# Modulation vectors made in the layer that uses them, and a feed-forward sum that is gated at its end

## The chip, the cores and the metric

The kernel runs on one core of a Trainium2 chip. The metric is the device time of one execution in microseconds (us), as the median of the runs shown. The engines are TensorE (PE, with its weight loads as PEld), VectorE (DVE), ScalarE (ACT), GpSimd (POOL) and SyncE (SP), whose queue issues all the DMAs that are spoken of here.

## What is computed

Two layers over 5 tiles of 128 tokens (one tile of context, four of latent tokens), 1024 wide. The reference of one layer, cut to what matters here:

```python
m = silu(cond) @ w_ada + b_ada
sh1, sc1, g1, sh2, sc2, g2 = split(m, 6)
h = layer_norm(x) * (1 + sc1) + sh1
o = mixing(h)            # state space | neighbourhood attention | grouped-query attention, then w_out
x = layer_norm(ALPHA * x + g1 * o, ln1_g, ln1_b)
h = layer_norm(x) * (1 + sc2) + sh2
a, gate = split(h @ w_ffn_in, 2)
f = (silu(a) * gate) @ w_ffn_out
x = layer_norm(ALPHA * x + g2 * f, ln2_g, ln2_b)
```

The context tile and the latent tiles have a conditioning vector each, so m has two rows. The six vectors of m are numbered 0 to 5 (sh1, sc1, g1, sh2, sc2, g2); "half" 0 or 1 is the first or last 512 columns of one.

## The kernel before

Matrix products are made in three matmuls of split operands (`mm3`, lines 311 to 313); `wload` and `wsplit` load a weight block by DMA into a buffer of the tag `wr` (three of them) and split it, a copy on ACT (line 283) and a subtraction on POOL or DVE (line 284), into buffers of the tags `wh` and `wl` (seven of each).

The order of the work is written as Python generators that a loop advances by tables of counts; a scheduler then orders each engine's instructions by priority and readiness. The stages of a layer are:

1. Mixers (`layer`, lines 1370 to 1448). 18 attention units of the grouped-query stage run in `pipelined`; after unit n the function `between` advances the state space mixer (`SSMN`), the remaining input projections (`WINN`) and the modulation (`ADAN`: one vector half after each of the units 6 to 11). Then follow 10 units of the neighbourhood attention.
2. Output projection (`wout`): two groups of tiles; after the second, `ADAW` advances three modulation steps. For each tile follow LayerNorm (`post_ln`), normalisation and the transposed input of the network. `xs[i]` is the tile after LayerNorm, in a `k4` buffer.
3. Feed-forward network (`ffn`): 22 column blocks f in six parts, `PARTS = (4, 4, 4, 3, 4, 3)`. Each block is `ffn_in` (products of 320 columns). After its blocks a part makes ten products of 512 columns (five tiles, two halves), each in one PSUM bank of `psA`, which takes the tags psM and psT in turn, two banks each. A product is multiplied by the gate row g2 (line 1755) and added to ALPHA * `xs[i]` (line 1757, part 0) or to `xs[i]` (line 1762). From f = 2 on, every block also advances `ffn_side` by one step: one modulation half (`ada_side`) and one step of the tables for the next layer's state space mixer (`ssm_tables`, lines 615 to 664).

One half of a modulation vector (`ada`, lines 361 to 401) loads eight row blocks of w_ada, 256 KB each, makes 32 matmuls (64 rows of the trace) into one PSUM bank, copies the bank's 128 columns on ACT (line 385), transposes the copy (line 386) and adds the bias on DVE (line 391 or 393). In the mixers the weights come two blocks at a time through `wr`; beside the network one at a time through `ev`, four buffers. For the gates the two rows go to DRAM (line 401), and `bcast_row` (line 406) reads them back to all partitions.

Layer 0's vectors 0 and 1 are made at the program's start, its vectors 2 to 4 in its mixers through the list `todo`. All later halves come from `ada_side`: vector 5 of the same layer, then vectors 0 to 4 of the next one, so that layer 1 has nothing to make in its mixers. That is 12 halves in layer 0, three in `wout` and nine beside the blocks f = 2 to 10.

## Time and profile before

| | us |
|---|---|
| median of 3 runs | 1804.81 |
| lowest and highest run | 1793.88, 1805.54 |
| the profiled execution | 1804.75 |
| its span, first to last instruction | 1802.7 |

Rough stages in the profiled execution: layer 0's mixers to 396 us, its projection to 460, its network to 990; layer 1's mixers to 1281, its projection to 1350, its network to the end. The parts of a network are cut where the sum of a part's last product begins (line 1762).

How to read the rows: a row of a table of windows has the stretch (start:end), its length, then for PE, PEld, DVE, ACT and POOL the busy us with the number of instructions, the mean granted clock of TensorE as a share of 2.4 GHz, the share of time in which the DMA engines are busy, and GB/s. A window taken for one line has PE and PEld of that line alone. A row of a group of instructions has line, engine, operation, result and operands, shape and count, then busy us and mean ns of one, then the idle time of the engine just before them and what ended it. A row of one line's instructions has the count, then the duration in ns (least, median, most), and the first and last start. Names such as wa, ev, psM are the tiles of the program.

### The profile page before, as it was taken

Reading aid. Unit: us, or ns where it says so; the run is one execution under the profiler, and the core shown is the slowest. Engines: PE = TensorE matmul, PEld = TensorE weight load, DVE = VectorE, ACT = ScalarE, POOL = GpSimd, SP = SyncE. Lnnn points to the kernel's source line nnn. Section 1 sums busy time; section 2 is a strip of 40 time slices with the busy share of each in tenths; the row PEclk is TensorE's granted clock in tenths of the full one; section 3 lists DMA queues with packets and bytes.
Section 4 is the critical chain, followed back from the end, with each engine's and each line's share of the span. In section 5 each row is a group of like instructions: output and inputs, shape, how many; then the busy total and the mean of one; then the engine's idle time right before and its main releaser. Section 6 shows DMA issues by size and latency. Waiting matters only on the chain.

```text
span 1802.7 us, 31473 instructions
## 1 busy us (share of the span) xinstructions
PE 1655.2 (92%) x11624; PEld 1447.3 (80%) x11624; DVE 1224.2 (68%) x2460; ACT 822.3 (46%) x1796; POOL 762.5 (42%) x651
## 2 busy tenths in 40 slices
PE   5889899898899999999898989998979999999997
PEld 3778677676688888898797978976759898998995
DVE  5576536646778777678877555565476787876777
ACT  5435445556542334243246446665564342432433
POOL 3753303048434334346266232210684464363453
PEclk8889899889899999999999989998989999999999
DMA  8434767545453545332324243463542232222312
GB/s 311 121 110 116 231 202 203 149 158 178 149 161 115 176 126 184 109 115 72 122 77 165 91 115 86 121 183 113 178 161 83 91 98 64 89 74 68 105 60 82
DMA packets 183114, 234.90 MB, mean 130 GB/s; under 512 B 78960, under 2 KB 112048, under 8 KB 182960
## 3 DMA queue, kind: packets, MB, share of 16 engines
q1 hardware_dynamic: 182960, 232.88, 42.3%
q8 instruction: 92, 1.51, 0.3%
q14 instruction: 62, 0.51, 0.1%
HBM read 203.57 MB, written 29.39 MB: 129 GB/s over the span
## 4 chain that ended last, share of the span: by engine, by line
PE 66%; DVE 12%; DMA 10%; ACT 4%; issue 3%; POOL 2%; SPq 1%; POOLq 0%; DVEq 0%; ACTq 0%
PE psM L311 9%; PE psM L312 9%; PE psM L313 9%; PE psT L311 6%; PE psT L312 6%; PE psT L313 5%; DMA ev<-in_w_ada_dram 3%; PE psT L859 3%; PE psS L311 2%; PE psS L312 2%; PE psS L313 2%; PE psS L1157 2%; DMA wr<-in_w_ffn_in_dram 2%; PE psT L1184 2%; POOL wl L284 2%
## 5 line engine op out<-in xcount | busy, mean ns | idle before, releaser
L284 POOL TENSOR_TENSOR wl<-wr,wh 128x512 fp32r<-128x512 f32 x362 | 502.1, 1406 | 523.8 <-ACT wh L283 341.6
L283 ACT CAST wh<-wr 128x512 fp32r<-128x512 f32 x450 | 275.0, 620 | 388.4 <-PE psM L313 91.3
L311 PE MATMUL psM<-hh,wh 128*128 128x320 f32 x560 | 178.1, 318 | 2.5 <-DVE ev L400 1.2
L312 PE MATMUL psM<-hl,wh 128*128 128x320 f32 x560 | 176.2, 315 | 0.3 <-POOL hl L284 0.3
L313 PE MATMUL psM<-hh,wl 128*128 128x320 f32 x560 | 176.2, 315 | 0.0
L311 PEld LDWEIGHTS psM<-hh,wh 128*128 128x128 f32 x560 | 107.1, 191 | 5.5 <-DVE ev L400 1.8
L311 PE MATMUL psT<-hh,wh 128*128 128x320 f32 x352 | 110.0, 312 | 0.0
L312 PE MATMUL psT<-hl,wh 128*128 128x320 f32 x352 | 109.1, 310 | 0.0
L313 PE MATMUL psT<-hh,wl 128*128 128x320 f32 x352 | 109.0, 310 | 0.0
L313 PEld LDWEIGHTS psM<-hh,wl 128*128 128x128 f32 x560 | 107.0, 191 | 1.7 <-issue 1.6
L312 PEld LDWEIGHTS psM<-hl,wh 128*128 128x128 f32 x560 | 107.2, 191 | 1.1 <-POOL hl L284 0.6
L230 POOL TENSOR_TENSOR sm<-sm,mhalf 128x1 f32<-128x1 f32 (+2 forms) x46 | 55.9, 1217 | 96.3 <-DVE sm L260 51.7
L1638 DVE TENSOR_TENSOR ys<-ys,psM 128x320 f32<-128x320 f32 x140 | 65.0, 482 | 34.7 <-PE psM L313 32.9
L1638 DVE TENSOR_TENSOR ys<-ys,psT 128x320 f32<-128x320 f32 x140 | 65.1, 481 | 30.4 <-PE psT L313 29.0
L1160 DVE TENSOR_REDUCE psS<-psS 128x1 f32<-128x640 f32 x64 | 52.8, 828 | 45.3 <-PE psS L1157 43.7
L311 PE MATMUL psT<-b,wh 128*128 128x320 f32 x240 | 76.6, 319 | 7.3 <-DVE ys L1638 7.2
L311 PE MATMUL psM<-b,wh 128*128 128x320 f32 x240 | 76.4, 318 | 5.7 <-DVE ys L1638 5.6
L284 POOL TENSOR_TENSOR wl<-ws,wh 128x512 fp32r<-128x512 f32 x40 | 53.6, 1341 | 62.7 <-ACT wh L283 62.6
L311 PE MATMUL psM<-wh,hh 128*128 128x256 f32 (+1 forms) x232 | 73.8, 318 | 6.1 <-DVE sm L1329 2.9
L311 PE MATMUL psM<-wh,xs 128*128 128x512 f32 x190 | 75.1, 395 | 3.5 <-DVE k L1762 2.8
L311 PE MATMUL psT<-wh,xs 128*128 128x512 f32 x190 | 75.3, 396 | 2.9 <-DVE k L1762 2.9
L859 PE MATMUL psT<-ident,ys 128*128 128x128 f32 x440 | 75.4, 291 | 2.7 <-ACT ys L290 1.0
(439 smaller groups left out, 4904.8 us busy)
## 6 DMA issues: line engine op xcount, KB each, us to landing
wr<-in_w_ffn_in_dram SPq DMA_DIRECT2D x88, 512.0 KB, 3.8
ev<-in_w_ada_dram SPq DMA_DIRECT2D x112, 256.0 KB, 4.0
wr<-in_w_ffn_out_dram SPq DMA_DIRECT2D x40, 512.0 KB, 3.9
wr<-in_w_out_dram SPq DMA_DIRECT2D x32, 512.0 KB, 3.6
wr<-in_w_in_dram SPq DMA_DIRECT2D x28, 512.0 KB, 4.4
wa<-in_w_ada_dram SPq DMA_DIRECT2D x24, 512.0 KB, 4.6
k<-in_x_dram SPq DMA_DIRECT2D x10, 512.0 KB, 5.6
xs<-zqk SPq DMA_DIRECT2D x32, 160.0 KB, 5.1
```

Of the source, the lines that this page charges most:

```text
L230: self.nc.gpsimd.tensor_tensor(out=o, in0=v, in1=self.mhalf.broadcast_to([128, v.shape[1]]), op=ALU.pow)
L283: nc.scalar.copy(hi, src)
L284: (lo_eng or nc.vector).tensor_tensor(out=lo, in0=src, in1=hi.bitcast(F32), op=ALU.subtract)
L311: nc.tensor.matmul(ps, lhsT=ah, rhs=bh, start=first, stop=False)
L312: nc.tensor.matmul(ps, lhsT=ah, rhs=bl, start=False, stop=False)
L313: nc.tensor.matmul(ps, lhsT=al, rhs=bh, start=False, stop=last)
L859: self.nc.tensor.transpose(pt[:, j * 128:(j + 1) * 128], s, self.ident)
L1157: nc.tensor.matmul(sp[:, b, 0:320], lhsT=qT[:, h * 128:(h + 1) * 128], rhs=kx[kv][:, b * 320:(b + 1) * 320], start=st, stop=en)
L1160: V.tensor_reduce(out=m, in_=sp[:, :, 0:320], axis=AX.XY, op=ALU.max, negate=True)
L1184: nc.tensor.matmul(pt[hh * 64:hh * 64 + 64, 256:384], lhsT=K["v"][:, j, kv * 64:kv * 64 + 64], rhs=PTs[j // 2][:, c0:c0 + 128], start=(j = ...
L1638: V.tensor_tensor(out=o, in0=x, in1=y, op=ALU.add)
```

## The change

Four edits go together.

- Vectors 2 to 4 of each layer are made in that layer's own mixers (`todo` is filled anew for each layer), and `ada_side` makes only vectors 0 and 1 of the next layer. Beside layer 0's network three halves are left (f = 2 to 4).
- In the mixers the new generator `ada_parts` makes a half in parts. A step of it computes the part whose weights the step before loaded, and loads the next. A part has two blocks of w_ada in the grouped-query stage, through `wr`, and up to four in the neighbourhood stage, through the buffers `wh` and `wl`. Each part has its own PSUM bank, ACT copy, transpose and DVE addition into `modc`. With 13 steps after the units 5 to 17 and up to 11 beside the neighbourhood units that makes 19 parts for a layer.
- The network's sum starts from zero, not from ALPHA * x, and without the gate: part 0 is copied by ACT, parts 1 to 3 are added by DVE. Part 4 fetches x from DRAM, in a buffer of the tag `zt` (two of them), adds, multiplies by the gate and adds ALPHA * x. Part 5 is as before.
- To that end every tile after LayerNorm is stored to a DRAM tile `xd` in `wout`. The gate rows are read when part 4 first needs them.

```diff
-    ADAN = (0,) * 6 + (1,) * 6 + (0,) * 6
+    ADA0 = 5
...
+    def ada_parts(self, l, M, todo):
...
+        for vec, half in todo:
+            c0 = vec * D + half * 512
+            mc = modc[:, vec, half * 4:half * 4 + 4, :]
+            k0 = 0
+            while k0 < KD:
+
+                n = 4 if self.ada_free else 2
+                n = min(n, KD - k0)
+                if self.ada_free:
+                    raws = [self.wp.tile([128, 512], F32, name=self.nm("wa"), tag=("wh", "wl")[j % 2], bufs=self.NW)
+                            for j in range(n)]
+                    for j, raw in enumerate(raws):
+                        nc.sync.dma_start(raw, wv[:, k0 + j, c0:c0 + 512])
+                else:
+                    raw = self.wp.tile([128, n, 512], F32, name=self.nm("wa"), tag="wr", bufs=self.NRAW)
+                    nc.sync.dma_start(raw, wv[:, k0:k0 + n, c0:c0 + 512])
+                    raws = [raw[:, j] for j in range(n)]
+                yield
+                bank = self.psM()
+                ps, pt = bank[:, 0:128], bank[:, 128:256]
+                for k in range(n):
+                    for j in range(4):
+                        nc.tensor.matmul(ps[32 * j:32 * j + 32, :], lhsT=self.silc[:, k0 + k, :],
+                                         rhs=raws[k][:, j * 128:(j + 1) * 128], start=(k == 0), stop=(k == n - 1),
+                                         tile_position=(0, 32 * j))
+                mrow = self.zt(128)
+                nc.scalar.copy(mrow, ps)
+                nc.tensor.transpose(pt, mrow, self.ident)
...
+                if k0:
+                    nc.vector.tensor_tensor(out=mc, in0=got, in1=mc, op=ALU.add)
+                else:
+                    nc.vector.scalar_tensor_tensor(out=mc, in0=got, scalar=float(vec in (1, 4)), in1=bc, op0=ALU.add,
+                                                   op1=ALU.add)
+                k0 += n
...
-            for _ in range(self.ADAN[n]):
-                if todo:
-                    self.ada(l, M, *todo.pop(0))
+            if n >= self.ADA0:
+                next(ada, None)
...
+        self.ada_free = True
         Ns = [self.na_prep(l, 0, zqk[0], znv)]
...
+            if n:
+                next(ada, None)
-        for _ in ssm:
+        for _ in itertools.chain(ada, ssm):
             pass
...
+                nc.sync.dma_start(xd[i], xs[i])
                 self.ffn_in_tile(xn, i, M["modc"], H)
...
-        for key, cd in (("gp", 0), ("gs", 1)):
-            row(key, M["gates"][1, cd])
...
-                g = row("gp", M["gates"][1, 0]) if i == 0 else row("gs", M["gates"][1, 1])
-                t = ps
-                V.tensor_tensor(out=t, in0=ps, in1=g[:, cs], op=ALU.mult)
+                x = xs[i][:, cs]
                 if part == 0:
-                    V.scalar_tensor_tensor(out=xs[i][:, cs], in0=xs[i][:, cs], scalar=ALPHA, in1=t, op0=ALU.mult,
-                                           op1=ALU.add)
-                elif last:
-                    self.residual(xs[i][:, cs], t, sums[n])
+                    S.copy(x, ps)
+                elif part < len(PARTS) - 2:
+                    V.tensor_tensor(out=x, in0=ps, in1=x, op=ALU.add)
                 else:
-                    V.tensor_tensor(out=xs[i][:, cs], in0=xs[i][:, cs], in1=t, op=ALU.add)
+                    g = row("gp", M["gates"][1, 0]) if i == 0 else row("gs", M["gates"][1, 1])
+                    if last:
+                        V.tensor_tensor(out=ps, in0=ps, in1=g[:, cs], op=ALU.mult)
+                        self.residual(x, ps, sums[n])
+                    else:
+                        t = self.zt()
+                        nc.sync.dma_start(t, xd[i][:, cs])
+                        V.tensor_tensor(out=ps, in0=ps, in1=x, op=ALU.add)
+                        V.tensor_tensor(out=ps, in0=ps, in1=g[:, cs], op=ALU.mult)
+                        V.scalar_tensor_tensor(out=x, in0=t, scalar=ALPHA, in1=ps, op0=ALU.mult, op1=ALU.add)
...
-            for vec in range(5):
+            for vec in range(2):
...
-            todo = [(2 + n // 2, n % 2) for n in range(6)]
             for l in range(L):
+                todo = [(2 + n // 2, n % 2) for n in range(6)]
```

The diff leaves the order of an engine's instructions to the scheduler, so three places of it follow. The first is PE in layer 1's neighbourhood stage, before: L859 and L978 are the transposes and the value products of an attention unit, L853 spreads its sums, L916 and L942 are scores, L767 is the state space mixer.

```order
L859 MATMUL psT_13526<-ident,ys_13339 128x128 x2
L859 MATMUL psT_13578<-ident,ev_13571 128x128 x2
L978 MATMUL psT_13526<-ys_13519,xs_13289 64x128 x4
L978 MATMUL psT_13526<-ys_13519,k_2439_13283 64x128 x2
L853 MATMUL psT_13526<-ident,sm_13355 64x128 x2
L767 MATMUL psS_13626<-k_2464_13374,k_2465_13375 80x128
L942 MATMUL psS_13662<-b_2490_13544,b_2489_13543 128x256
```

And PE at the same place with the change, ahead of the same step of the state space mixer (now L818); L427 and L432 are the matmuls and the transpose of a modulation part, wa its weights.

```order
L427 MATMUL psM_13557<-wa_13505,silc 32x128 x4
L427 MATMUL psM_13557<-wa_13506,silc 32x128 x4
L427 MATMUL psM_13557<-wa_13507,silc 32x128 x4
L427 MATMUL psM_13557<-wa_13508,silc 32x128
L432 MATMUL psM_13492<-ident,zt_13501 128x128
L427 MATMUL psM_13557<-wa_13508,silc 32x128 x3
L818 MATMUL psS_13669<-k_2495_13342,k_2496_13343 80x128 x8
L821 MATMUL psS_13669<-k_2494_13341,k_2220_11888 80x128 x2
L910 MATMUL psT_13652<-ident,ys_13398 128x128 x2
```

A whole part of four blocks has come in between, and the transpose of the part before it, each with a bank psM of its own.

The second place is DVE at the products of part 4 in layer 1, before: one multiplication (L1755) and one addition (L1762) for each product.

```order
L1755 TENSOR_TENSOR psT_18311<-psT_18311,k_2736_14773 128x512
L1755 TENSOR_TENSOR psM_18326<-psM_18326,k_2736_14773 128x512
L1762 TENSOR_TENSOR k_2655_14370<-k_2655_14370,psT_18311 128x512
L1755 TENSOR_TENSOR psT_18341<-psT_18341,k_2735_14771 128x512
L1762 TENSOR_TENSOR k_2653_14367<-k_2653_14367,psM_18326 128x512
L1762 TENSOR_TENSOR k_2575_13975<-k_2575_13975,psT_18341 128x512
L1755 TENSOR_TENSOR psM_18356<-psM_18356,k_2736_14773 128x512
```

And with the change, the same products on DVE: addition (L1821), gate (L1822), and ALPHA * x from the loaded row zt (L1823).

```order
L1821 TENSOR_TENSOR psT_18395<-psT_18395,k_2717_14496 128x512
L1821 TENSOR_TENSOR psM_18415<-psM_18415,k_2715_14493 128x512
L1822 TENSOR_TENSOR psT_18395<-psT_18395,k_3438_18408 128x512
L1821 TENSOR_TENSOR psT_18433<-psT_18433,k_2637_14098 128x512
L1822 TENSOR_TENSOR psM_18415<-psM_18415,k_3438_18408 128x512
L1823 SCALAR_TENSOR_TENSOR k_2717_14496<-zt_18410,psT_18395 128x512
L1822 TENSOR_TENSOR psT_18433<-psT_18433,k_3443_18446 128x512
L1821 TENSOR_TENSOR psM_18453<-psM_18453,k_2635_14095 128x512
L1823 SCALAR_TENSOR_TENSOR k_2715_14493<-zt_18428,psM_18415 128x512
L1822 TENSOR_TENSOR psM_18453<-psM_18453,k_3438_18408 128x512
```

Three instructions stand for a product where two did, and a bank is free after the third.

The third place is the SP queue at the end of layer 0's part 4, before: wr are the weights of the blocks f = 19 (9931, 9933) and f = 20 (10079, 10081).

```order
L1582 DMA wr_9931<-in_w_ffn_in_dram 128x1024
L1582 DMA wr_9933<-in_w_ffn_in_dram 128x1024
L406 DMA k_1976_10493<-in_ln_b_dram 128x1024
L664 DMA tabC_5862<-ev_9729 128x2x256
L664 DMA tabC_5862<-ev_9734 128x2x256
L1582 DMA wr_10079<-in_w_ffn_in_dram 128x1024
L1582 DMA wr_10081<-in_w_ffn_in_dram 128x1024
```

And the SP queue there with the change; wr_9838 and wr_9840 are the weights of f = 20, and zt the rows of x. The first two of the ten row loads stand far ahead, at the network's start.

```order
L715 DMA tabC_5951<-ev_9459 128x2x256
L1820 DMA zt_9539<-xd_4523 128x512
L1820 DMA zt_9557<-xd_4523 128x512
L1820 DMA zt_9575<-xd_4523 128x512
L1639 DMA wr_9838<-in_w_ffn_in_dram 128x1024
L1820 DMA zt_9613<-xd_4523 128x512
L1820 DMA zt_9631<-xd_4523 128x512
L1820 DMA zt_9649<-xd_4523 128x512
L1820 DMA zt_9667<-xd_4523 128x512
L1820 DMA zt_9685<-xd_4523 128x512
L1059 DMA zt_10841<-in_qkg_dram 128x128
L1639 DMA wr_9840<-in_w_ffn_in_dram 128x1024
```

Eight row loads now stand ahead of the second load for f = 20; each of them waits until DVE has freed a buffer zt. A small load of the next stage (L1059) goes into zt as well.

## Rows read from the trace of the kernel before

**Rows 1.** Head of the page: span, and each engine's busy time and share.

```profile
span 1802.7 us, 31473 instructions
PE 1655.2 (92%) x11624; PEld 1447.3 (80%) x11624; DVE 1224.2 (68%) x2460; ACT 822.3 (46%) x1796; POOL 762.5 (42%) x651
```

**Rows 2.** Windows: layer 0's parts 0, 1, 2, 4; layer 1's part 1.

```profile
468.00:565.00 97.00, 90.63 (x660) 80.25 (x660) 72.55 (x194) 38.58 (x76) 32.15 (x25) 0.97 0.43 137
565.00:662.00 97.00, 92.55 (x717) 79.31 (x716) 74.69 (x134) 33.73 (x70) 37.32 (x29) 0.98 0.57 161
662.00:761.00 99.00, 98.86 (x732) 84.50 (x732) 68.08 (x105) 34.21 (x67) 40.38 (x30) 1.00 0.44 135
...
825.00:915.00 90.00, 80.78 (x457) 74.66 (x456) 75.48 (x113) 29.24 (x57) 39.39 (x29) 0.96 0.31 100
...
1437.00:1514.00 77.00, 76.36 (x453) 71.14 (x453) 58.74 (x88) 28.86 (x56) 37.47 (x29) 1.00 0.26 83
```

**Rows 3.** Windows of line 381 alone, layer 0's parts 1 and 2.

```profile
565.00:662.00 97.00, 11.41 (x254) 5.83 (x254) 0.98 0.57 161
662.00:761.00 99.00, 9.88 (x192) 4.09 (x192) 1.00 0.44 135
```

**Rows 4.** Groups of instructions, 565 to 761 us, and line 386's own row.

```profile
L381 PE MATMUL psS<-ev,silc 128*32 128x128 f32 x446 | 21.3, 282 | 4.3 <-DMA ev<-in_w_ada_dram 4.2
...
L386 PE MATMUL psS<-ident,ev x9: 270/272/272, 522.4 to 750.7; 128*128 128x128 f32 x9
```

**Rows 5.** Groups of instructions on PE, 662 to 761 us: the tables.

```profile
L631 PE MATMUL psS<-k,ev 128*128 128x32 f32 x32 | 4.7, 280 | 0.0
...
L655 PE MATMUL psS<-ident,ev 128*128 128x128 f32 x16 | 2.4, 272 | 0.0
```

**Rows 6.** Windows in the mixers of both layers.

```profile
1052.00:1175.00 123.00, 116.95 (x1029) 105.27 (x1030) 69.85 (x185) 76.33 (x196) 27.05 (x35) 0.96 0.38 104
1175.00:1281.00 106.00, 98.39 (x657) 77.02 (x656) 58.66 (x151) 61.80 (x163) 23.38 (x26) 0.89 0.55 160
...
1200.00:1255.00 55.00, 48.23 (x297) 36.45 (x296) 35.19 (x97) 31.37 (x91) 5.67 (x10) 0.78 0.53 145
...
141.00:313.00 172.00, 156.68 (x1588) 134.24 (x1590) 97.44 (x226) 89.16 (x223) 47.72 (x55) 0.97 0.66 193
1067.00:1194.00 127.00, 124.77 (x1141) 112.53 (x1140) 75.71 (x198) 81.58 (x210) 27.54 (x38) 1.00 0.39 107
```

**Rows 7.** Groups on PE, 181 to 276 us: layer 0's six halves.

```profile
L381 PE MATMUL psM<-wa,silc 128*32 128x128 f32 x384 | 18.1, 280 | 5.1 <-DMA wa<-in_w_ada_dram 5.0
...
L386 PE MATMUL psM<-ident,zt 128*128 128x128 f32 x5 | 1.6, 313 | 3.1 <-ACT zt L385 3.1
```

**Rows 8.** Lines 1755 and 1762; window of ten products in layer 1.

```profile
L1755 DVE TENSOR_TENSOR psM<-psM,k x50: 686/695/700, 544.4 to 1730.7; 128x512 f32<-128x512 f32 x50
...
L1762 DVE TENSOR_TENSOR k<-k,psM x40: 628/681/689, 641.4 to 1731.4; 128x512 f32<-128x512 f32 x40
...
1711.00:1731.00 20.00, 20.00 (x91) 16.64 (x90) 15.04 (x22) 4.61 (x8) 5.62 (x5) 1.00 0.08 27
```

**Rows 9.** Loads of w_ada (line 377) to landing; one DMA issue.

```profile
DMA to landing us min/median/max: 2.5/4.4/8.0
...
xmid<-k SPq DMA_DIRECT2D x5, 512.0 KB, 2.6
```

**Rows 10.** POOL's group, 300 to 318 us; window of layer 0's projection.

```profile
L284 POOL TENSOR_TENSOR wl<-wr,wh 128x512 fp32r<-128x512 f32 x4 | 5.5, 1410 | 0.8 <-ACT wh L283 0.8
...
396.00:460.00 64.00, 55.42 (x332) 42.06 (x331) 41.52 (x90) 38.05 (x71) 51.99 (x42) 0.89 0.55 179
```

**Rows 11.** Groups on PE, 141 to 313 us: the tables in layer 0's mixers.

```profile
L631 PE MATMUL psS<-k,k 128*128 128x32 f32 x32 | 4.5, 268 | 0.0
...
L655 PE MATMUL psS<-ident,k 128*128 128x128 f32 x20 | 3.1, 278 | 0.4 <-ACT ev L658 0.4
```

**Rows 12.** Line 381, 396 to 480 us: PE idle before it (us, times).

```profile
  DMA ev<-in_w_ada_dram: 12.1, 7
```

More of the change, by code (lines that the diff above doesn't have):

```diff
@@ L1 @@
+import itertools
 import math
@@ L394, in ada @@
         if vec in (2, 5) and half == 1:
-            gc = self.smallp.tile([128, 2, KD], F32, name=self.nm("gc"), tag="gc", bufs=1)
-            nc.vector.tensor_copy(gc, modc[:, vec].rearrange("p k c -> p c k"))
-            pt = bank[0:16, 256:384]
-            nc.tensor.transpose(pt, gc.rearrange("p c k -> p (c k)"), self.ident)
-            row = (self.ev(n=128) if side else self.zt(128))[0:16]
-            nc.vector.tensor_copy(row, pt)
-            nc.sync.dma_start(gates[vec // 3].rearrange("c (k p) -> (c k) p", p=128), row)
+            self.gate_rows(M, vec, bank, self.ev if side else self.zt)
@@ new lines, in gate_rows @@
+    def gate_rows(self, M, vec, bank, place):
+        nc = self.nc
+        gc = self.smallp.tile([128, 2, KD], F32, name=self.nm("gc"), tag="gc", bufs=1)
+        nc.vector.tensor_copy(gc, M["modc"][:, vec].rearrange("p k c -> p c k"))
+        pt = bank[0:16, 256:384]
+        nc.tensor.transpose(pt, gc.rearrange("p c k -> p (c k)"), self.ident)
+        row = place(n=128)[0:16]
+        nc.vector.tensor_copy(row, pt)
+        nc.sync.dma_start(M["gates"][vec // 3].rearrange("c (k p) -> (c k) p", p=128), row)
@@ L1417, in between @@
                     preps[n + self.AHEAD][0](preps[n + self.AHEAD][1])
+        ada = self.ada_parts(l, M, todo)
         self.pipelined(units, 1, between)
@@ L1470, in wout @@
         ada = self.ada_side(l, M, nxt)
+        xd = self.dp.tile([NT, 128, D], F32, name=self.nm("xd"))
         self.function(AF.Silu, self.after)
```

13 lines of the change are left out of this document (11 added, 2 removed).

## Prediction

> **What bounds the kernel now.** The head of the page says that TensorE (PE) is busy for 1655.2 of 1802.7 us and VectorE (DVE) for 1224.2 [rows 1]. That is a mean over stages, so the windows come next. In layer 1's network, part 1 (1437 to 1514 us) has PE busy for 76.36 of 77 us and DVE for 58.74: PE sets the pace, and whatever leaves DVE there is worth nothing [rows 2]. The same products in layer 0 take 97 us (part 1) and 99 us (part 2) [rows 2]. Looking for the extra 42 us, I took the matmuls of the modulation vectors (line 381) alone: 11.41 us in part 1 and 9.88 us in part 2 [rows 3]. One half of a vector is 64 matmul rows, so these are 4 and 3 halves, 20.2 and 21.3 us / 7 = 3.0 us each. PE also idled for 4.2 us in the two parts until their weights had landed [rows 4], and in part 2 the tables for the next layer's state space mixer add 4.7 + 2.4 us of PE [rows 5]. The rest is PE waiting for a DVE that is busier than in layer 1 (74.69 us against 58.74). In part 4 of layer 0 the tables make DVE the limit: PE 80.78, DVE 75.48 of 90 us [rows 2].
>
> The mixers of layer 1, where six halves are to go, look full too: PE 116.95 of 123 us, then 98.39 of 106 [rows 6]. But weight loads (PEld) fill 86% and 73% there, and in the network's saturated part 71.14 of 77 us, 92% [rows 2, 6]. Measured by that, the first stretch has 123 x 0.92 - 105.27 = 8 us of room and the second 106 x 0.92 - 77.02 = 20 us. From 1200 to 1255 us the mean granted clock was 0.78, so part of that stretch ran at the lower of the two levels, 1.2 GHz [rows 6].
>
> **The change, part by part.** The profiled execution took 1804.75 us for its span of 1802.7, and the median of the runs shown is 1804.81; the sum is made against 1804.75.
>
> (A) Layer 0's network loses six of its nine remaining vector halves, three each from parts 1 and 2. Matmuls: 3/4 of 11.41 plus 9.88 = 18.4 us. Six transposes at 0.27 [rows 4] = 1.6. Idle for weights: 6/7 of 4.2 = 3.6. Parts 1 to 3 also lose one of their two DVE instructions for every product (0.68 us [rows 8], ten products a part), so DVE falls by 7 us a part. Of the PE waits that remain in parts 1 and 2 I take 2.4 us. Sum -26. Bounds: -18 (matmuls alone) and -32 (both parts down to layer 1's 77 us plus one half, 3 us, and the tables' 7).
>
> (B) Layer 1's mixers gain those six halves, in 19 loads and as many transposes and DVE additions where a half had one. The nearest row is layer 0, which makes its six in its own mixers: 18.1 us of matmuls, 5.1 us idle for weights [rows 7]. Transposes: 19 x 0.31 = 6 us. The upper bound is 18.1 + 5.1 + 6 = 29, nothing hidden. The lower is -4: all of it in the room above, and a higher clock from 1200 to 1255. The loads now go out one step ahead, so the 5.1 goes; 24 us remain, and I let half of the 28 us of room take 13. Value +11.
>
> (C) Layer 0's mixers keep their six halves, with 13 transposes more (4 us) and without the wait for weights (-5.1); about three halves move into the later stage, where PEld has room. Value -3, between -10 (half of the matmuls hidden) and +8 (the transposes and their waits in full).
>
> (D) Part 4 in both layers: every product now needs three DVE instructions and a row load where it had two. Over its ten products PE needs 20 us and DVE was busy for 15.04 [rows 8]; ten times 0.68 us makes 22. Besides, ten loads of 256 KB pass through two buffers: a buffer is free after the third DVE instruction, and is wanted again two products (4.0 us) later. Loads of that size landed after 2.5 us at least and 4.4 in the median [rows 9], so the loop takes 3.2 or 5.1 us. With 5.1, four rounds lose 4.4 us. PE can run ahead by the four PSUM banks that these products take in turn. Value +7 for both layers, between 0 and +14. On the SP queue one load of the next weights (f=20) is now behind eight row loads; it is wanted only after f=19's products, (77 - 20) / 4 = 14 us on, so I charge nothing; if that cover were gone it would be one landing a layer, for which I take the median of 4.4 us [rows 9].
> The Trainium skill (DMA: Bandwidth & Descriptors, Anatomy of one DMA) gives a transfer some 2.0 us of fixed time plus its bytes at 436 GB/s, which is an estimate of 2.6 us for 256 KB. This case's fastest load, 2.5 us [rows 9], agrees; the median does not. By that page alone the loop would never bind, and (D) would be 4 us less.
>
> (E) Part 0 in layer 0 moves ten evacuations to ACT (busy for 38.58 of 97 us) and drops twenty DVE instructions (13.6 us of 72.55) [rows 2]; part 3 drops ten. PE was short of work there only now and then: -2, between 0 and -5. In layer 1 the same edits are worth 0, as DVE already keeps up there.
>
> (F) Five stores of 512 KB per layer to DRAM, each behind its LayerNorm on the SP queue. The like stores to xmid landed in 2.6 us [rows 9]. Behind the fourth and fifth store stand loads of modulation weights, for which PE idles 12.1 us in that stage of layer 0 already [rows 12]; a store that waits, or that shares the DMA engines, makes them later. +3 for both layers, between 0 and +8.
>
> (G) The output projection's first weights used to be split early, in idle time of POOL (GpSimd): four at 300 to 318 us, 5.5 us [rows 10]. Now the buffers hold modulation weights at that time, and these four fall to the start of the projection, where POOL is busy for 51.99 of 64 us. +3 for both layers, between 0 and +11.
>
> Sum: -26 + 11 - 3 + 7 - 2 + 3 + 3 = -7, so 1797.75, called 1798 us.
>
> **The rivals.** First, the mixers swallow everything. The tell is PEld: 105.27 of 123 us leaves more than PE's 116.95 suggests. Then B is 0, C -6, D +4 and G +1: -26 + 0 - 6 + 4 - 2 + 3 + 1 = -26, 1779 us. Against it: six of the 19 pieces come before a PE queue that is in order, and each transpose waits for an ACT copy.
> By the Trainium skill (Perfetto Trace Analysis, Identifying the Most-Contended Engine) headroom of TensorE is judged by LDWEIGHTS busy and not by matmul busy, which would favour this rival; the trace agrees in the network, where 92% goes with no waits, and no run here shows yet whether the room in the mixers can be used.
>
> Second, slower: a bank of PSUM becomes the bound of the mixers. The tag psM has two banks, and every one of the 19 pieces holds one from its first matmul over the ACT copy and the transpose to the DVE addition; the projection tiles and the state space steps, which fill PE between attention units, need the same two. For it: the grouped-query stage took 172 us in layer 0, which had six halves in it, and 127 us in layer 1 [rows 6], 45 more. The tables' matmuls explain 4.5 + 3.1 us of this [rows 11]. If the other 37 belong to the modulation, B is +37 and the sum -7 + 26 = +19: 1824 us. It makes the kernel slower from B = 18 on, and by over 1% from B = 36. Against it: in layer 0 that stage also had tables on DVE and a DMA share of 0.66.
>
> Third, the saving in layer 0 is real, but part 4's loop costs its upper bound and the stores and weights too: D +14, F +6, G +6: -7 + 7 + 3 + 3 = +6, 1811 us. And as far as the ungated sum was to relieve DVE in layer 1, it can do nothing there, since PE is full; that is already in the sum.
>
> **How the numbers follow.** Chances: forecast 0.48, swallowed 0.25, bank-bound 0.17, part 4's loop 0.10. A measurement of this kernel can tell about 1% (18 us) from no change; so the first rival is faster, the forecast (own range 1787 to 1811) and the third are within, the second is slower. Giving a little of the forecast's lower side to faster: 0.26, 0.57, 0.17. The range takes in most of the first rival and reaches to the second: 1775 to 1822. All lower bounds together would give -51, all upper +52; that they fall together is unlikely.
>
> **What would show it.** Parts 1 and 2 of layer 0 should last 82 to 90 us instead of 97 and 99, with 64 rows of modulation matmuls in part 1 and none in part 2. Layer 1's stretch from its first attention unit to the projection should grow by 5 to 17 us; by 0 the first rival is right, by 30 or more the second. In part 4, DVE waiting for the rows from DRAM shows the loop (D). The forecast is wrong if parts 1 and 2 keep over 92 us (then DVE or the tables, not the vectors, held them), or if layer 0's mixers change by more than 10 us either way.

## The result and the profile after

The changed kernel took 1821.04 us (median of 8 runs, 1816.99 to 1826.36), the kernel before 1807.23 us beside it (8 runs, 1793.88 to 1812.52): a ratio of 1.008, with a 95% interval of 1.0051 to 1.011. It is slower by 14 us where 7 us less were forecast. All ratios below are to the kernel before on the same chip. The profiled executions differ by nearly the same (spans of 1815.7 and 1802.7 us), so the two traces can be set side by side.

The head of the page of the changed kernel ([rows 1] of before):

```profile
span 1815.7 us, 31583 instructions
PE 1651.3 (91%) x11650; PEld 1444.9 (80%) x11650; DVE 1176.5 (65%) x2406; ACT 834.4 (46%) x1842; POOL 765.7 (42%) x651
```

DVE lost 48 us of work and PE 4, and the program got longer: what matters is where. The stages are cut at starts of instructions: the last gated product of the output projection (the multiplication by the gate in `wout`), and in a part the last copy, first addition or gate multiplication of its ten products.

| stage (profiled execution, us) | before | after | difference |
|---|---|---|---|
| start to layer 0's last gated projection | 442.5 | 443.5 | +1.0 |
| layer 0, parts 1 and 2 | 196.0 | 178.1 | -17.9 |
| layer 0, part 4 | 90.1 | 95.3 | +5.2 |
| layer 0, parts 0, 3 and 5 | 258.9 | 250.1 | -8.8 |
| **layer 1's mixers**, to its last gated projection | 339.1 | 377.4 | **+38.3** |
| layer 1, part 4 | 76.9 | 79.2 | +2.3 |
| layer 1, the other parts and the end | 399.2 | 392.1 | -7.1 |

Windows of the changed kernel: layer 0's parts 1, 2 and 4, layer 1's parts 1 and 3. The first four answer to [rows 2] (columns as there):

```profile
561.00:654.00 93.00, 87.77 (x550) 78.52 (x549) 68.59 (x118) 31.96 (x66) 40.70 (x29) 0.96 0.38 106
654.00:739.00 85.00, 83.14 (x512) 77.10 (x511) 60.84 (x95) 31.39 (x62) 39.29 (x29) 1.00 0.29 88
802.00:897.00 95.00, 81.36 (x460) 74.79 (x460) 82.40 (x121) 29.41 (x57) 40.87 (x29) 0.96 0.36 117
1453.00:1530.00 77.00, 76.55 (x455) 71.32 (x454) 51.82 (x77) 29.27 (x57) 36.94 (x28) 1.00 0.25 82
1608.00:1666.00 58.00, 57.34 (x340) 53.22 (x339) 40.16 (x61) 21.45 (x42) 28.76 (x22) 1.00 0.25 83
```

Part 3 of layer 1 before, the one row of it that no group shows:

```profile
1592.00:1654.00 62.00, 59.04 (x340) 54.38 (x340) 44.90 (x71) 21.45 (x42) 28.50 (x22) 0.97 0.24 77
```

In layer 1's part 1, DVE fell from 58.74 us to 51.82 and the 77 us stayed: PE is the limit there. In part 3, with three blocks to a product instead of four, the lighter DVE gave 4 us. Part 4 of layer 0 has DVE busy for 82.40 of 95 us.

Layer 1's mixers, the window of the kernel before and that of the changed one:

```profile
987.50:1326.60 339.10, 318.82 (x2347) 274.96 (x2346) 193.74 (x477) 195.13 (x470) 110.42 (x108) 0.93 0.44 130
```

```profile
967.00:1344.40 377.40, 340.40 (x2774) 287.55 (x2773) 201.49 (x501) 201.11 (x492) 114.07 (x111) 0.94 0.51 154
```

PE is busy for 21.6 us more and idle (length less busy time) for 37.0 us instead of 20.3. The groups of the parts in layer 1 (968 to 1345 us; [rows 7] of before shows the halves in layer 0):

```profile
L427 PE MATMUL psM<-wa,silc 128*32 128x128 f32 x384 | 17.2, 290 | 1.2 <-ACT k L767 1.2
...
L432 PE MATMUL psM<-ident,zt 128*128 128x128 f32 x19 | 5.5, 290 | 2.0 <-ACT zt L431 2.0
```

These 22.7 us are about the busy time that was added. The idle time in front of the parts' own instructions is 3.2 us; the rest of the 17 us of idle time stands elsewhere.

### The profile page after: what moved, and what is told of

It reads as the page before. It is cut to its first block, busy times and chain, and to the rows that moved or that the text cites. A ratio compares the mean times of both kernels' runs of the same rounds, so it can differ in the third digit from the quotient of the medians.

```text
span 1815.7 us, 31583 instructions
## 1 busy us (share of the span) xinstructions
PE 1651.3 (91%) x11650; PEld 1444.9 (80%) x11650; DVE 1176.5 (65%) x2406; ACT 834.4 (46%) x1842; POOL 765.7 (42%) x651
## 4 chain that ended last, share of the span: by engine, by line
PE 63%; DVE 15%; DMA 9%; ACT 5%; POOL 4%; issue 4%; SPq 1%; POOLq 0%; DVEq 0%; ACTq 0%
PE psM L312 9%; PE psM L313 8%; PE psM L314 8%; PE psT L312 6%; PE psT L313 5%; PE psT L314 5%; DMA wr<-in_w_ffn_in_dram 3%; PE psT L910 3%; POOL wl L285 2%; PE psS L1208 2%; PE psS L314 2%; PE psS L312 2%; PE psS L313 2%; PE psT L1235 2%; DMA ev<-in_w_ada_dram 2%
## 5 line engine op out<-in xcount | busy, mean ns | idle before, releaser
L1645 DVE TENSOR_TENSOR ws<-wr,wr 128x512 f32<-128x512 f32 x40 | 34.1, 853 | 88.8 <-DMA wr<-in_w_ffn_in_dram 45.7
```

Source lines behind the costliest of these rows:

```text
L1645: V.tensor_tensor(out=o, in0=x, in1=y, op=op)
```

## The experiments

"Layer 1's mixers" is the fifth row of the table. Its times are from one profile a kernel; in three other runs that leave its code alone (the sum alone, with ev, and the last one below) they were 339, 337 and 341 us, and the neighbourhood stage alone 81 to 89 us. (With the gate at the end, where the cut ahead of the stage falls later, they were 326.) A few us there are scatter, and the ratios (medians of several runs) carry the verdicts.

**Which half of the change costs.** The move alone, with the sum of before:

```diff
+                t = ps
+                V.tensor_tensor(out=t, in0=ps, in1=g[:, cs], op=ALU.mult)
                 if part == 0:
-                    S.copy(x, ps)
```

> The modulation vectors are moved as in the changed kernel; the network's sum, its gate rows and the missing row stores are those of the kernel before. Theory 1 (TensorE's work is paid wherever it stands: the mixers of layer 1 lose 38 us, the network of layer 0 wins 18, layer 0's mixers are even): about 19 us slower than before, ratio 1.010, and layer 1 from its last network product to its last gated projection longer by 30 to 40 us. Theory 2 (the loss comes from the new sum, its stores and row loads): ratio 0.997 to 1.002.

Measured: 1.0094 (1.0065 to 1.0124), layer 1's mixers 380.7 us. The sum alone, in the kernel before:

```diff
+                nc.sync.dma_start(xd[i], xs[i])
...
                 if part == 0:
...
+                    S.copy(x, ps)
```

> The modulation vectors stay as before; the network's sum is the ungated one, with row stores and row loads. Theory 1: parts 0, 3 and 5 gain, part 4 loses, as between the two traces: 4 us less in each layer, ratio 0.994 to 0.998, layer 1's mixers as long as before within 3 us. Theory 2: ratio 1.005 to 1.010, with layer 1's mixers or projections longer.

Measured: 0.9957 (0.9934 to 0.9979), layer 1's mixers 339.0 us. The move is the loss and the sum a gain of 8 us; the stores cost nothing that shows (the projections' times changed by +0.5 and -0.6 us).

**What of a part costs.** Half the rows, all else kept:

```diff
-                for k in range(n):
+                for k in range(1):
```

> The changed kernel, in which each part multiplies only the first of its two to four blocks of modulation weights (the vectors 2 to 4 come out incomplete); loads, banks, ACT copies, transposes and DVE additions stay. It leaves out 2 x 232 of 768 matmul rows of 42 ns. Theory 1: the time falls by their 20 us, to a ratio of 0.995 to 1.000 against before. Theory 3 (a PSUM bank held over copy and transpose bounds the mixers): the bank is held as long but for 0.4 us a part, so the time falls by 0 to 6 us, ratio 1.005 to 1.009.

Measured: 1.0028 (1.0005 to 1.0051), between both theories; layer 1's mixers 379.5 us, no shorter. The neighbourhood stage of layer 1, in this run and in the changed kernel:

```profile
1206.00:1305.00 99.00, 89.59 (x574) 67.36 (x569) 52.89 (x131) 54.61 (x144) 31.24 (x29) 0.84 0.58 174
```

```profile
1206.00:1307.00 101.00, 89.58 (x729) 67.50 (x728) 50.41 (x132) 55.71 (x145) 31.01 (x29) 0.90 0.63 198
```

PE is busy for the same 89.6 us with 155 rows fewer, at a mean granted clock of 0.84 instead of 0.90 of 2.4 GHz: more of the rows that stayed ran at the level of 1.2 GHz. That the missing rows brought this about is not shown. In five kernels that leave the stage's code alone (before, the sum alone, with ev, with the gate at the end, the last one) its clock was between 0.85 and 0.89, and layer 0's neighbourhood stage went the other way in these two runs, from 0.85 with all rows to 0.90 with half. The profiled execution also took 1816.26 us, where the median of this run is 1811.15. By the medians half of the rows are worth 9 us, not the 20 of their time.

One transpose a half:

```diff
-                mrow = self.zt(128)
-                nc.scalar.copy(mrow, ps)
-                nc.tensor.transpose(pt, mrow, self.ident)
+                if k0 == 0:
+                    acc = self.wp.tile([128, 512], F32, name=self.nm("ws"), tag="ws", bufs=1)[:, 0:128]
+                    nc.scalar.copy(acc, ps)
                 else:
+                    nc.vector.tensor_tensor(out=acc, in0=ps, in1=acc, op=ALU.add)
+                if k0 + n == KD:
+                    nc.tensor.transpose(pt, acc, self.ident)
```

> The changed kernel, in which the parts of a half are summed untransposed in one buffer in SBUF (ACT copies the first part, DVE adds the others) and only the last part is transposed: 6 transposes a layer in place of 19. Theory 1 with the waits at the transposes as the second cost: in layer 1, 13 of 19 transposes with their 3.6 us and 6.4 us of idle time behind them go, 7 us; both layers 10 to 14 us, ratio 1.000 to 1.003. If the transposes' waits are only a symptom of the mixers' chains: 0 to 5 us, ratio 1.005 to 1.008.

Measured: 1.0026 (1.0002 to 1.005), layer 1's mixers 371.5 us, in the first of the two ranges: 10 us of the program. Another bank:

```diff
-                bank = self.psM()
+                bank = self.psT()
```

> The changed kernel, in which a part takes its PSUM bank from the tag psT (attention transposes and values) and leaves psM to the projections and the state space mixer. 'Layer 1's mixers' is the time from the last product of layer 0's network to the last gated product of layer 1's output projection: 339 us before, 377 with the change. Theory 3 (the two psM banks bound the mixers): down by 10 us or more in each layer, ratio 0.995 to 1.000. Other theories: within 5 us of the changed kernel, ratio 1.004 to 1.011.

Measured: 1.0121 (1.0082 to 1.016); layer 1's mixers took 371.5 us, but layer 0 reached its last gated projection 14 us later. Theory 3, the second rival's mechanism, is not borne out: away from psM the kernel is not faster. The attention uses psT, so this run alone does not clear the banks. In the changed kernel PE waited 0.6 us in all in layer 1's mixers for a bank that a part's addition freed, and 4.1 us in layer 0's.

Then parts of the work were taken out whole. Loads and buffers alone:

```diff
-                bank = self.psM()
...
                 for k in range(n):
...
-                nc.tensor.transpose(pt, mrow, self.ident)
...
+                    nc.scalar.copy(self.spare, raws[k][:, 0:1])
```

> The changed kernel, in which the parts of the vectors 2 to 4 keep their loads and buffers (each block is released by a copy of one column on ACT, a step later), but leave out matmuls, copies, transposes and additions; the vectors hold the bias alone. Theory 4 (the loads and the buffers wr, wh, wl, that they take from the weights of the projections, make the mixers longer): layer 1's mixers stay above 360 us. Theory 1 (TensorE's work and the waits around it): 340 to 350 us, and layer 0's mixers shorter than before by 20 us or more.

Measured: 0.9867 (0.9832 to 0.9903), layer 1's mixers 356.5 us, between the two. It decides nothing: the added ACT copies stood in front of the attention's own, and ACT waited for loads:

```profile
ACT spare L425 <- DMA wa<-in_w_ada_dram: 31.0, 21, 3.8
```

All but the loads, with the resident identity as the weights:

```diff
-                    nc.sync.dma_start(raw, wv[:, k0:k0 + n, c0:c0 + 512])
...
-                                         rhs=raws[k][:, j * 128:(j + 1) * 128], start=(k == 0), stop=(k == n - 1),
+                                         rhs=self.ident, start=(k == 0), stop=(k == n - 1),
```

> The changed kernel, in which the parts of the vectors 2 to 4 multiply the resident identity in place of loaded weights: all matmuls, banks, copies, transposes and additions, but no load and no buffer. Theory 4: layer 1's mixers 340 to 355 us. Theory 1: 365 to 380 us.

Measured: 0.9968 (0.9951 to 0.9985), layer 1's mixers 360.8 us. Both theories have a share: 16.6 us go with the loads, 21.7 stay. The same with the first block only:

```diff
-                for k in range(n):
+                for k in range(1):
```

> The run without loads, in which each part also multiplies only its first block (it leaves out 2 x 232 of 768 matmul rows of 42 ns). There the 21.7 us that layer 1's mixers keep over before should be TensorE's work: if so they fall by 7 to 10 us, to 351 to 354, ratio 0.985 to 0.992. If a chain over copy, transpose and addition paces the parts instead: by less than 4 us, ratio 0.994 to 0.998.

Measured: 0.9992 (0.9969 to 1.0015), layer 1's mixers 366.6 us, a miss of both ranges: here half of the rows are worth nothing. Matmuls alone, without hand-overs:

```diff
-                nc.scalar.copy(mrow, ps)
-                nc.tensor.transpose(pt, mrow, self.ident)
...
+                if k0 == 0:
+                    nc.vector.tensor_copy(mc, bc)
```

> The run without loads, in which the parts of the vectors 2 to 4 keep only their matmuls, on the resident identity, each part into its own bank of psM; it leaves out the loads, ACT copies, transposes and DVE additions, and the vectors hold the bias alone. Without loads layer 1's mixers took 361 us, 339 before. Theory 1 (TensorE's time for the parts is what remains): 352 to 358 us, 16 us of matmuls on top of 339. Theory 7 (the hand-overs from PE to ACT, PE and DVE, each in order with the attention behind them, are what remains): 338 to 346 us.

Measured: 0.9870 (0.9845 to 0.9895), layer 1's mixers 357.2 us, as theory 1 has it. Nothing at all, and half of the matmuls:

```diff
-                for k in range(n):
-                    for j in range(4):
-                        nc.tensor.matmul(ps[32 * j:32 * j + 32, :], lhsT=self.silc[:, k0 + k, :],
```

> The changed kernel without any work for the vectors 2 to 4 in the mixers: no loads, no matmuls, no copies, transposes or additions (the vectors hold the bias alone). It is the zero point of the runs that keep a part of it: matmuls alone 357 us in layer 1's mixers, matmuls and hand-overs 361, everything 377. Theory 1 (TensorE's time of the matmuls is paid in full): 337 to 343 us, as before the change, ratio 0.972 to 0.978. If the rest of the change (stores, later weights) lengthens this stage by itself: 348 us or more, and the matmuls cost less than their time.

```diff
-                for k in range(n):
+                for k in range(1):
```

> The run with matmuls alone, halved: each part multiplies its first block only, no loads, no hand-overs; 2 x 232 rows of 42 ns less, 10 us a layer. Theory 1: layer 1's mixers 347 to 350 us, ratio 0.976 to 0.983. If the number of parts counts and not their length, as halving them suggested twice: 355 to 359 us, ratio 0.985 to 0.989.

Measured: 0.9717 (0.9682 to 0.9753) with layer 1's mixers at 341.5 us, and 0.9824 (0.9797 to 0.9852) with 354.3. The zero point is that of before, so nothing else of the change lengthens the stage. The runs now form a ladder of steps. Layer 1's mixers with no parts, with matmuls alone, and with matmuls and hand-overs, a window of each kernel:

```profile
929.50:1271.00 341.50, 315.53 (x2371) 272.91 (x2370) 197.17 (x481) 199.47 (x475) 115.04 (x111) 0.95 0.46 134
```

```profile
951.70:1308.90 357.20, 332.28 (x2752) 282.36 (x2751) 203.97 (x483) 197.13 (x474) 114.20 (x111) 0.96 0.44 128
```

```profile
967.70:1328.50 360.80, 337.32 (x2770) 287.47 (x2770) 202.10 (x502) 202.48 (x493) 115.39 (x111) 0.95 0.43 127
```

| step (ratios x 1807 us; both layers, twelve halves) | from | to | us | of it in layer 1's mixers |
|---|---|---|---|---|
| matmuls | 0.9717 | 0.9870 | 27.6 | 15.7 |
| copy, transpose, addition | 0.9870 | 0.9968 | 17.7 | 3.6 |
| loads | 0.9968 | 1.0080 | 20.2 | 16.6 |

The matmuls add 16.75 us to PE's busy time in layer 1 and 15.7 to the stage, and PE's idle time stays (26.0 and 24.9 us): nothing hides them. The loads add 3 us of busy time but 13.5 of idle time (23.5 to 37.0). The intervals of the ratios leave 5 to 8 us of doubt on each step of the program. In layer 0, to its last gated projection, the profiles give 408.0 us with no parts, 425.2 with matmuls alone, 441.7 with hand-overs and 443.5 with everything: 17.2 us for the matmuls, 16.5 for the hand-overs, 1.8 for the loads. So the matmuls cost both layers about the same, the hand-overs fall on layer 0 and the loads on layer 1. Why the hand-overs cost that much in layer 0 is not shown; PE's 4.1 us of waits for banks there are a part of it at most.

What the half-matmul runs say is less clear. By the medians 19 of the 27.6 us come with the first 152 rows of 384 a layer, where 11 would be in proportion, and the doubt is 8 us. The 354.3 us of the stage are from a profiled execution of 1781.71 us, where the median is 1771.85, and are too long if anything. Whether a part costs something beside its rows stays open.

**What the loads cost.** ACT's and DVE's waits for DMA in layer 1 from the first grouped-query score to the first neighbourhood score (1035.0 to 1205.8 us) of the changed kernel: the waiting instruction, what ended the wait, us in all, times, longest:

```profile
ACT b L928 <- DMA xs<-zqk: 6.2, 2, 5.6
...
ACT wh L284 <- DMA wr<-in_w_in_dram: 4.1, 3, 2.3
...
DVE xs L1132 <- DMA xs<-zq: 5.2, 4, 2.8
DVE modc L438 <- PE psM L432: 4.3, 2, 3.7
```

Before, ACT waited 1.2 us for DMA in that stretch and DVE 1.8; now 12.3 with two smaller rows, and 5.2. The use of the buffers wr there shows why (lines with wr in that stretch, before, then after: operation, count, duration, first and last start):

```profile
L301 SPq DMA_DIRECT2D wr<-in_w_out_dram x5: 333/333/457, 1122.2 to 1196.9; - x5
L301 SPq DMA_DIRECT2D wr<-in_w_in_dram x3: 332/333/1437, 1058.0 to 1080.1; - x3
```

```profile
L302 SPq DMA_DIRECT2D wr<-in_w_in_dram x4: 333/339/417, 1100.6 to 1157.6; - x4
L302 SPq DMA_DIRECT2D wr<-in_w_out_dram x1: 341/341/341, 1201.7 to 1201.7; - x1
```

The last w_in loads go out at 1157.6 instead of 1080.1 us (123 and 28 us into the stretch). A part holds one of three buffers wr until PE has come to it; ACT splits the weights of the projections, in order, and the attention's copies and exponentials stand behind. The rows zq and zqk are the projections' results and are late with them. Two runs tell buffers from the queue:

```diff
-                    raw = self.wp.tile([128, n, 512], F32, name=self.nm("wa"), tag="wr", bufs=self.NRAW)
-                    nc.sync.dma_start(raw, wv[:, k0:k0 + n, c0:c0 + 512])
+                    raws = [self.ev() for j in range(n)]
+                    for j, raw in enumerate(raws):
+                        nc.sync.dma_start(raw, wv[:, k0 + j, c0:c0 + 512])
```

> The changed kernel, in which the parts of the grouped-query stage load into two of the four buffers ev, so that the three buffers wr belong to the projections' weights again. Theory 5 (the parts keep the projections' weights out of wr, and ACT, in order, waits for them with the attention behind): layer 1 from its first grouped-query score to its first neighbourhood score, 171 us with the change and 145 before, falls by 8 us or more, ratio 1.000 to 1.005. Theory 6 (the issue queue SP, in order, stands behind the parts' loads): within 4 us of the changed kernel, ratio 1.006 to 1.011.

```diff
-                        nc.sync.dma_start(raw, wv[:, k0 + j, c0:c0 + 512])
+                        nc.gpsimd.dma_start(raw, wv[:, k0 + j, c0:c0 + 512])
...
-                    nc.sync.dma_start(raw, wv[:, k0:k0 + n, c0:c0 + 512])
+                    nc.gpsimd.dma_start(raw, wv[:, k0:k0 + n, c0:c0 + 512])
```

> The changed kernel, in which the loads of all parts of the vectors 2 to 4 are issued by GpSimd in place of SP; the buffers stay. Theory 6: layer 1 from its first grouped-query score to its first neighbourhood score falls by 8 us or more, and ACT no longer waits there for rows zqk and weights of w_in; ratio 1.000 to 1.005. Theory 5: within 4 us, ratio 1.006 to 1.011.

Measured: 1.0078 (1.0051 to 1.0106) through ev, 1.0108 (1.0085 to 1.0132) on the other queue. ACT's waits for DMA in the same stretch, through ev and then on the other queue:

```profile
ACT b L929 <- DMA xs<-zqk: 1.3, 1, 1.3
ACT zt L431 <- DMA zqk<-zt: 1.2, 1, 1.2
ACT sm L1278 <- DMA out_na_v_dram<-sm: 1.1, 1, 1.1
```

```profile
ACT b L928 <- DMA xs<-zqk: 5.7, 1, 5.7
...
ACT wh L284 <- DMA wr<-in_w_in_dram: 4.3, 3, 2.7
```

With ev the waits for weights are gone and the stretch is 10.1 us shorter (170.8 to 160.7; without any loads it took 158.3), so theory 5 holds for it. On the other queue the waits stay, yet the stretch is 6.9 us shorter, between the two ranges; these runs do not explain that. But the ratio through ev did not move: the neighbourhood stage behind took 107.0 us instead of 101.0, for as many rows of PE at a granted clock of 0.82 instead of 0.90. Whether ev caused this lower clock is not shown, as there is one profile of each. Both cures together:

```diff
-                    raw = self.wp.tile([128, n, 512], F32, name=self.nm("wa"), tag="wr", bufs=self.NRAW)
+                    raws = [self.ev() for j in range(n)]
...
+                if k0 + n == KD:
+                    nc.tensor.transpose(pt, acc, self.ident)
```

> The changed kernel with both cures: the parts of the grouped-query stage load into ev, and a half is summed in SBUF and transposed once. If the two costs add up (10 us for wr in the grouped-query stretch, 6 us for transposes in layer 1's mixers, as each run alone showed): layer 1's mixers 355 to 363 us, ratio 0.998 to 1.002. If a later stage gives back what the first wins, as with ev alone: 368 to 377 us, ratio 1.003 to 1.009.

Measured: 0.9973 (0.9953 to 0.9994), layer 1's mixers 360.1 us. The stage is where the sum of the two costs had it. In the program the cures win 19 us together, where ev alone won 0.4 and one transpose a half alone 10; what makes the pair worth more is not shown. This kernel is faster than before the change, by 5 us. It is at the level of the run without loads (0.9968, 360.8 us), and of the 18.6 us that its mixers of layer 1 keep over the run with no parts the matmuls alone cost 15.7.

**Part 4 and the sum.** Row loads in four buffers, on the kernel with the sum alone:

```diff
-                        t = self.zt()
+                        t = self.ev()
```

> The modulation as before, the ungated sum, and part 4's row loads in the four buffers ev in place of the two of zt. If the loop over two buffers costs part 4 (theory D of the prediction): part 4 2 to 5 us shorter in layer 0 than in the run with the sum alone (94.9 us), 1 to 2 in layer 1 (79.2 us), ratio 0.991 to 0.995. If DVE's three instructions cost it: within 1 us, ratio 0.994 to 0.998.

Measured: 0.9988 (0.9959 to 1.0017), above both ranges. Part 4 of that run and of the one with the sum alone:

```profile
822.20:917.20 95.00, 83.27 (x463) 76.75 (x462) 81.73 (x122) 29.99 (x57) 40.32 (x29) 0.95 0.38 122
```

```profile
822.70:917.60 94.90, 83.17 (x463) 76.66 (x463) 82.08 (x121) 30.09 (x57) 40.23 (x29) 0.95 0.37 117
```

The two buffers did make DVE wait for rows (2.0 us in this part of the run with the sum alone, 2.4 us in the changed kernel); with four these waits are gone, and part 4 is as long. What stayed is PE's wait for a bank that DVE's third instruction frees. Here are PE's waits for banks of the products in layer 0's part 4: before (line 1762 is the second instruction), with the sum alone and with ev (line 1768 is the third):

```profile
PE psM L311 <- DVE k L1762: 2.5, 1, 2.5
```

```profile
PE psT L311 <- DVE k L1768: 4.9, 1, 4.9
```

```profile
PE psM L311 <- DVE k L1768: 4.9, 1, 4.9
```

The gate in the last part, as an edit of the run with the sum alone:

```diff
-                elif part < len(PARTS) - 2:
+                elif not last:
                     V.tensor_tensor(out=x, in0=ps, in1=x, op=ALU.add)
...
+                    V.scalar_tensor_tensor(out=x, in0=t, scalar=ALPHA, in1=ps, op0=ALU.mult, op1=ALU.add,
+                                           accum_out=sums[n])
```

> The modulation as before; the sum stays ungated through part 4, and the last part adds, multiplies by the gate and adds ALPHA times the stored row. If part 4's cost is DVE's three instructions: part 4 is 3 to 5 us shorter in layer 0 and 2 us in layer 1 than in the run with the sum alone (94.9 and 79.2 us), part 5 1 to 3 us longer, ratio 0.992 to 0.996. If part 4's cost is something else: part 4 as long, ratio 0.996 to 1.000.

Measured: 0.9951 (0.9923 to 0.9979). Its part 4:

```profile
815.60:903.60 88.00, 80.97 (x458) 74.84 (x458) 69.23 (x103) 29.49 (x56) 39.34 (x28) 0.96 0.30 96
```

6.9 us shorter with DVE at 69.23 us instead of 82.08, and PE waits for no bank of a product: DVE's instructions are part 4's cost. (The row loads left part 4 with them, but the run with ev had shown that their buffers did not bind.) In exchange layer 0's part 5 and the stretch up to layer 1's first score took 6.6 us more; in layer 1 part 4 won 2.4 us and part 5 lost 7.2. It is as good as the sum alone and no better.

**A version of the best parts.** Layer 1's vectors beside layer 0's network as before, layer 0's in parts through ev with one transpose a half:

```diff
-                todo = [(2 + n // 2, n % 2) for n in range(6)]
+                todo = [(2 + n // 2, n % 2) for n in range(6 * (l == 0))]
```

> A version put together from what the runs showed: the ungated sum; layer 1's vectors 2 to 4 beside layer 0's network, as before the change; layer 0's, which have to be made in its mixers, in parts through ev with one transpose a half. Layer 1's mixers 336 to 342 us. If the parts serve layer 0 better than its six whole halves did (438 us to its last gated projection with parts in ev and one transpose, 439 to 446 with whole halves in four runs): ratio 0.990 to 0.994. If they are as good: 0.995 to 0.998.

Measured: 0.9999 (0.9977 to 1.0022), above both ranges. In layer 0 parts are no better than whole halves; by the ratios this kernel is 8 us behind the sum alone (0.9957). The faster kernels are the sum alone (0.9957), with the gate at the end (0.9951), and the move with both cures (0.9973); these runs do not tell them apart.

## Why the prediction was wrong

The forecast was 7 us less and the measurement is 14 us more. The 1821.04 us lie inside the stated range of 1775 to 1822, at its very end: the range was drawn that wide towards the second rival, and the sum behind it had the wrong sign.

| term | forecast | measured | what the runs showed |
|---|---|---|---|
| A, parts 1 and 2 of layer 0 | -26 | -17.9 | its lower end, the matmuls alone |
| B, layer 1's mixers (with F and G there) | +11 | +38.3 | 15.7 matmuls, 3.6 hand-overs, 16.6 loads; 2.4 at the zero point |
| C, layer 0's mixers (with F and G there) | -3 | +1.0 | the halves cost what they did |
| D, part 4 of both layers | +7 | +7.5 | size right by luck, cause wrong |
| E and layer 1's sum | -2 | -15.9 | 8.8 in layer 0, of which 5.2 come with the move alone; 7.1 in layer 1 |
| F, stores; G, weights | +6 | about 0 | F: projections unchanged in the run with the sum alone; G: with the change they are 3.7 and 4.0 us shorter |

**The step that failed is (B)**: "The loads now go out one step ahead, so the 5.1 goes; 24 us remain, and I let half of the 28 us of room take 13." Neither half of it stood. The room was read from weight loads (PEld). In layer 1's mixers PEld filled 274.96 of 339.10 us, 81%, yet the matmuls lengthened the stage by 15.7 us for 16.75 us of busy time. The Trainium skill (Perfetto Trace Analysis, Identifying the Most-Contended Engine) judges headroom by MFU, the share of peak arithmetic, and LDWEIGHTS busy; the second of these, taken alone, led astray here, and the measurement decides. In this stage of many short matmuls PE's busy time of 318.82 of 339.10 us was the better sign. And the loads did not become free by going out earlier: a load that goes out early holds a buffer longer. The nearest row for this price was there, in the use of wr by the projections, and I did not ask who else needs the three buffers.

The bounds of (B) failed with it. Its upper end, 29, was read from layer 0, where the loads cost next to nothing: to its last gated projection layer 0 took 441.7 us without them and 443.5 with. In layer 1 they cost 16.6. The 6 us that the prediction gave to transposes are not a fixed price either: the hand-overs cost 16.5 us in layer 0 and 3.6 in layer 1.

**(A)** had the matmuls right (17.9 us for six halves, 3.0 each) and added 7.6 us for transposes, for weights and for DVE that were not gained. The move alone shortens the two parts by 17.2 us and the sum alone by 5.3, both together by 17.9: the gains do not add, as the prediction's sum has it. PE's idle time in parts 1 and 2 was 4.6 us before (97.00 - 92.55 and 99.00 - 98.86) and 7.1 after. Part 1 kept 93 us, which the prediction named as a sign against it: 16 matmuls of the tables (line 682), none of which ran there before, moved into it from part 2:

```profile
L682 PE MATMUL psS<-k,ev x16: 268/276/401, 630.9 to 633.8; 128*128 128x32 f32 x16
```

**(D)** came out at 7.5 for a forecast of 7, but that is luck: the loop over two buffers was not its cause; DVE's third instruction was. The 4.4 us of landing time were read from loads of w_ada, 512 KB ones among them [rows 9]. The row loads themselves (line 1820 of the changed kernel) were faster:

```profile
DMA to landing us min/median/max: 2.4/2.7/5.5
```

With 2.7 us in place of 4.4 the prediction's own loop takes 3.4 us, less than the 4.0 it had, and does not bind; four buffers changed part 4 by 0.1 us. The estimate from the Trainium skill (DMA: Bandwidth & Descriptors, Anatomy of one DMA), 2.6 us, by which the loop never binds, was the better one, though that section gives it for transfers that GpSimd issues and these go out by SP. What hangs on that rule, a (D) smaller by 4 us, did not come: part 4 still lost 5.2 and 2.3 us, to DVE's instructions, and not the 3 that the sum left for them.

**(E)** undervalued DVE where a part has three blocks: "In layer 1 the same edits are worth 0" holds for parts 1 and 2 (-0.2 and 0.0 us), but part 3 won 3.9 us, as the windows above show (the granted clock rose from 0.97 to 1.00 and PE idles 0.66 us instead of 2.96). The run with the sum alone has this gain too (62.5 to 58.5 us), the one with the move alone has not. In layer 0 the term is about 3 us rather than 8.8, as parts 0, 3 and 5 are 5.2 us shorter with the move alone.

**The rivals.** The second one gave 1824 us, nearly the measured time, and its sign came true: from the first attention unit to the projection layer 1 took 272.0 us instead of 232.8. But the reason was another one, and so the nearness is in part luck. In layer 1 all the hand-overs, with the banks held over them, cost 3.6 us; only layer 0's 16.5 us leave room for a bank. Its arithmetic took the 37 us by which layer 0's grouped-query stage exceeds layer 1's for the price of six halves. With no halves in either, the stretch from the first grouped-query score to the first neighbourhood score still took 163.2 us in layer 0 and 145.0 in layer 1, so only some 25 of the 43 us between them (188.5 and 145.2 before) were the halves'. The price of six halves in a mixer was near 37 all the same: with no parts layer 0 reached its last gated projection after 408.0 us instead of 442.5, 34.5 us for six whole halves. That neighbour was worth more than the room by which it was argued away. The first rival, that the mixers swallow all, is refuted by the ladder; the third by the runs with the sum.

## What to carry to other kernels

A half of a vector cost 3.0 us beside the network and 5.5 us in the mixers ((1.0080 - 0.9717) x 1807 us / 12): moving work of a busy engine into a stage that looks less full pays only if the engine's idle time there can be filled, and the price of the same work where it already stands in such a stage (here layer 0's) is the best forecast of it. Price a move by leaving the work out first, then adding matmuls, hand-overs and loads one by one; and ask of every buffer that the moved loads use who prefetches through it. An edit that only lightens an engine beside it can be the better half of a change: here the sum alone wins 8 us that the move hid. And set a stage time from a profile beside the median of its run before a theory hangs on it.

## What the runs showed that was not expected

Halving the matmuls of the parts gave less than their time: 9 us of 20 with everything else kept (1.0080 to 1.0028), and nothing without loads (0.9968 to 0.9992), while leaving out the hand-overs gave 17.7 us over both layers. The clock of the neighbourhood stage fell in the first of these runs and not in the second, so it does not explain both.

The same work was not paid for in the same place in the two layers: the hand-overs cost 16.5 us in layer 0's mixers and 3.6 in layer 1's, the loads 1.8 and 16.6.

A cure in one stage was given back in the next: 10.1 us less in the grouped-query stretch through ev, 6.0 us more in the neighbourhood stage, at a lower granted clock. One transpose a half alone gave 10 us of the program, ev alone nothing, and both together 19.
